# Six P.V matmuls per attention unit, and one cross product for both directions of retention

## The chip, the core and the metric

The kernel runs on one core of a Trainium2 chip. Its time is the device time of one execution, in microseconds; the number given for a kernel is the median of its runs. Five engines work side by side, each through its own instructions in order: TensorE (PE in the profile; its weight loads are shown as PEld), VectorE (DVE), ScalarE (ACT), GpSimd (POOL) and SyncE (SP). SP issues most loads. GpSimd issues nearly all stores, on its own queue, and does a little arithmetic. TensorE writes its results to PSUM, which is split into banks of 128 x 512 numbers; all other tiles lie in SBUF.

## The reference

One layer of an encoder on 1024 tokens of width 1024, in float32:

```python
x = x + 0.5 * post1(swiglu(pre1(x)))
u = pre_mix(x)
rq, rk, rv, rg, nq, nk, nv, g_ret, g_na = split(u @ w_mix_in)
y_ret = (silu(rg) * headnorm(fwd_retention + bwd_retention)) @ w_ret_out
y_na  = neighbourhood_attention(nq, nk, nv, rel_bias) @ w_na_out
x = x + post_mix((sigmoid(g_ret) * y_ret + sigmoid(g_na) * y_na) @ w_out)
x = x + 0.5 * post2(swiglu(pre2(x)))
```

Two parts matter here. **Neighbourhood attention** has 8 heads of 64 numbers on a grid of 16 rows by 64 columns of tokens; each query sees a window of 8 rows by 16 columns, with a bias, a softmax, and then P.V, the product of the probabilities with the values v. **Retention** has 4 heads (128 numbers in q and k, 256 in v). It goes through the sequence in 8 chunks of 128 tokens, forward and backward. Each direction carries a state S of 128 x 256; a chunk's output is an inner product within the chunk plus the *cross products* q.S of the two directions, each scaled by its decay.

## The kernel before

**High and low parts.** Every product is made with numbers split in two: `c.split(h, l, src)` (L62, L63) has ScalarE write the rounded high part and VectorE (or another engine given as `eng`) the rest, the low part. `c.mm3` (L92 to L96) then makes three matmuls into one bank: high.high (L94), high.low (L95), low.high (L96), so these three lines hold most of TensorE's work.

**Attention** (`na_cores`, L929) takes the heads in four pairs. A pair has 8 *units*, each a block of 8 x 16 = 128 queries with 12 x 32 = 384 keys, so there are 32 units; in the profile they run from about 973 us (the first scores) to 1145 us (the last result). A unit goes through three steps, in three consecutive turns of the loop (L1036 to L1059):

- `scores`: four matmuls (L983), the bias and the maximum (VectorE, L984, L986), the exponentials (ScalarE, L988), and the scaling by one over the sum (L990, L992).
- `flip`: `vload` brings the values of a column block when they are first needed and splits them into `vh` and `vl`, 16 times in all; six transposes (L1002) bring the keys onto the partitions, and the transposed probabilities are split into `pth` and `ptl`.
- `values`: P.V. The weights are `vh` or `vl` of one key block, 128 columns wide: 64 of the one head beside 64 of the other. The moving operand has the probabilities of both heads, 256 columns. So a matmul makes head against head, and half of its result, one head's values with the other's probabilities, isn't used. Three key blocks by three matmuls of `mm3` are nine matmuls per unit. ScalarE copies the two halves that count (64 rows each) into `ot` (L1018). After 8 units `ot` is stored to `no` in HBM.

Between these steps `fill(n)` makes the next steps of an independent generator (`products`, L1493): the projection of retention's v and the gate projections, one step being one `mm3` of 512 columns. They keep TensorE at work while a unit's softmax is made. TensorE's instructions have one order; so have the other engines'. The order on each engine is set when the program is built, by the framework's scheduler, which walks the program with a model of its times and takes the first instruction in the program's order that it thinks ready; so an instruction can stand earlier on its engine than in the text.

**Retention** (`ret_cores`, L1120) follows. Per head it walks the chunks backwards and keeps the backward states `sb` (`update`, L1167), and splits q and k (`split_qk`). Then it walks forwards: for each chunk the scores of the next (`scores`), the forward state (`update`), the split of the state (`state`), and then three groups of `mm3`: `cross[:, 256:]` with the backward state, `inner`, and `cross[:, :256]` with the forward state, each 256 columns wide. `norm` puts them together. The last chunk has no backward part and the first no forward part.

**Places.** A pool's tiles lie one behind the other in SBUF, in the order of their first mention, and pools that are opened one after another share the place. `reuse_waits="tile"` makes the first write to a new tile wait only for the old tiles that lay under it. So retention's tiles, at the place of attention's, wait for the last use of those; the lines of `pool.tile(...)` ahead of the loop (L1024 to L1032) and the `pad` tiles set which lies under which. `mix` is the pool below attention's. It holds the fill's output tiles (`ev`), the decay table `dec` and retention's gate tiles `rg`.

**The rotary part** (`rotate`, L1107), earlier in the kernel, is the one place that accumulates in HBM: it stores a tile, and then `swap` (L1115, L1116) adds other halves to it by `dma_start(..., accum_op=add)` on GpSimd's queue, which has to wait until the store has landed.

Of the kernel before, what the change touches and what calls it, by code (L numbers as in the profile page):

```python
# [19 lines left out]
P = 128  # L20
# [908 lines left out]
def na_cores(c, pool, d, bias, fill, n0, n1, n2, first, early):  # L929
# [32 lines left out]
    def vload(hp, cb):  # L962
        vr = pool.tile([P, 4, P], F32, tag="vraw", name="vraw", bufs=1)
        vh = pool.tile([P, 4, P], F32R, tag="vh", name="vh", bufs=2)
        vl = pool.tile([P, 4, P], F32R, tag="vl", name="vl", bufs=2)
        nc.sync.dma_start(vr, d["nvg"][cb][:, :, hp * P:(hp + 1) * P].rearrange("t p d -> p t d"))
        c.split(vh, vl, vr)
        vop[hp, cb] = vh, vl
# [26 lines left out]
    def flip(s):  # L995
        pth = pool.tile([P, 6, P], F32R, tag="pth", name="pth", bufs=2)
        ptl = pool.tile([P, 6, P], F32R, tag="ptl", name="ptl", bufs=2)
        for g in range(2):
            pt = c.bank("pt", 2)
            for j in range(3):  # L1000
                i = 3 * g + j
                nc.tensor.transpose(pt[:, j * P:(j + 1) * P], s[:, i % 2, (i // 2) * P:(i // 2 + 1) * P], c.ident)  # L1002
            c.split(pth[:, 3 * g:3 * g + 3], ptl[:, 3 * g:3 * g + 3],
                    pt[:, :384].rearrange("p (k t) -> p k t", k=3))
        return pth, ptl

    def values(hp, rg, cb, pt):
        if hp not in ots:
            ots[hp] = pool.tile([P, 16, 64], F32, tag="ot", name="ot", bufs=2)
        ot = ots[hp]  # L1010
        po = c.bank()
        vh, vl = vop[hp, cb]
        for k in range(3):
            c.mm3(po[:, :256].rearrange("p (e t) -> p e t", e=2), (vh[:, rg + k], vl[:, rg + k]),
                  (pt[0][:, 2 * k:2 * k + 2], pt[1][:, 2 * k:2 * k + 2]), k == 0, k == 2)
        for e in range(2):
            es = slice(64 * e, 64 * e + 64)
            nc.scalar.copy(ot[es, 8 * rg:8 * rg + 8, 16 * cb:16 * cb + 16],  # L1018
                           po[es, e * P:(e + 1) * P].rearrange("p (r c) -> p r c", c=16))
# [4 lines left out]
    for q in ("pth", "ptl"):  # L1024
        pool.tile([P, 6, P], F32R, tag=q, name=q, bufs=2)
    pool.tile([P, 4, P], F32R, tag="vl", name="vl", bufs=2)
    pool.tile([P, 128], F32, name="pad")
    qload(0)
    load(0)
    pool.tile([P, 4, P], F32R, tag="vh", name="vh", bufs=2)  # L1030
    ots[0] = pool.tile([P, 16, 64], F32, tag="ot", name="ot", bufs=2)
    pool.tile([P, 1024], F32, name="pad2")  # L1032
# [3 lines left out]
    for i in range(n + 2):  # L1036
# [17 lines left out]
        if i >= 2:  # L1054
            hp, _, rg, cb = units[i - 2]
            values(hp, rg, cb, pt.pop(i - 2))
            if (i - 2) % 8 == 7:
                c.store(d["no"][hp], ots[hp].rearrange("p r c -> p (r c)"))
# [61 lines left out]
def ret_cores(c, pool, spool, d, dec, fill, n, early):  # L1120
# [55 lines left out]
    def state(st, b):  # L1176
        s = [pool.tile([P, 256], F32R, tag=f"s{b}{q}", name=f"s{b}{q}", bufs=2) for q in "hl"]
        c.split(*s, st)
        return s
# [531 lines left out]
```

## Time and profile before

| | |
|---|---|
| median of 3 runs | 2205.85 us (2205.7 to 2206.21) |
| span of the profiled execution | 2203.7 us |
| mean granted TensorE clock | 0.999 |
| P.V matmuls (L94, L95, L96), 256 columns | 3 x 96 |
| cross product matmuls, 256 columns | 6 x 28 |
| stores of `ot` | 4, landing after 3.2 / 3.3 / 8.5 us (least, median, most) |
| loads of v (`vraw`) | 16, landing after 2.7 / 3.4 / 10.5 us |

The profiled execution's span is the time from its first to its last instruction; the median holds 2.15 us more. A line of the profile that groups instructions reads: line, engine, operation, what it writes `<-` what it reads, partitions x elements, how many | busy us, mean ns of one | idle time before them, and what ended it. A line with three numbers parted by strokes has the least, the median and the longest duration in ns and the time of the first and the last. A line of the timeline reads: start in us, duration, engine, line, operation, and in square brackets the engine's idle time before it and what ended that. A line of the waits reads: who waited, for what, us in total, times. In the busy times by stretches each engine has its busy us and, in brackets, its instructions.

### The profile page before, as it was taken

What the parts mean: (1) busy time and instruction counts of PE and PEld (TensorE: products, weight loads), DVE (VectorE), ACT (ScalarE), POOL (GpSimd) and SP (SyncE); (2) the same over time, 40 slices, a digit from 0 to 9 for tenths busy, and PEclk for the clock granted to TensorE, in tenths of its full rate; (3) what the DMA queues carried; (4) which work ended last, traced back from release to release, by engine and by line L of the source; (5) the groups of instructions that cost most, each with busy time, mean ns of one, the idle gap of its engine ahead of it and who ended that gap; (6) DMA issues with size and microseconds to landing.
All of it is one profiled execution on the core that took longest, in us unless ns stands there. A gap on an engine that the chain in (4) does not pass through costs nothing.

```text
span 2203.7 us, 29707 instructions
## 1 busy us (share of the span) xinstructions
PE 2185.3 (99%) x10232; PEld 1824.9 (83%) x10232; DVE 1573.0 (71%) x2767; ACT 959.9 (44%) x1970; POOL 585.7 (27%) x766
## 2 busy tenths in 40 slices
PE   8999999999999999999999999999999999999998
PEld 7878888888888888888888888888888888888887
DVE  7898887655568767777766677644999787866444
ACT  7444444322344332367775564322644433433232
POOL 2121222169421113311001222101112121216942
PEclk9999999999999999999999999999999999999999
DMA  7354544597745556676553466785446343549865
GB/s 264 130 200 171 203 167 169 219 375 284 247 171 188 196 172 152 155 235 180 182 171 122 154 201 220 286 305 178 148 153 229 134 167 130 181 173 374 275 225 184
DMA packets 151206, 444.63 MB, mean 202 GB/s; under 512 B 19472, under 2 KB 46224, under 8 KB 148944
## 3 DMA queue, kind: packets, MB, share of 16 engines
q1 hardware_dynamic: 107456, 298.78, 39.9%
q0 software_dynamic: 43472, 139.77, 17.8%
q10 hardware_dynamic: 128, 4.19, 0.6%
q8 instruction: 81, 1.33, 0.2%
q14 instruction: 69, 0.57, 0.1%
HBM read 294.54 MB, written 152.32 MB: 203 GB/s over the span
## 4 chain that ended last, share of the span: by engine, by line
PE 91%; issue 3%; DVE 3%; DMA 1%; ACT 1%; POOL 1%; POOLq 0%; SPq 0%; DVEq 0%; ACTq 0%
PE ps L94 28%; PE ps L95 28%; PE ps L96 28%; PE pt L96 1%; PE pt L94 1%; PE pt L95 1%; PE ps L983 1%; PE pt L1002 1%; PE pt L133 0%; POOL rstd L104 0%; DMA no<-ot 0%; PE pt L1216 0%; DMA vl<-rv 0%; DMA gt<-in_dram 0%; DMA vraw<-nvg 0%
## 5 line engine op out<-in xcount | busy, mean ns | idle before, releaser
L63 DVE TENSOR_TENSOR wl<-wraw,wh 128x512 fp32r<-128x512 f32 x440 | 294.1, 691 | 50.6 <-ACT wh L62 49.9
L62 ACT CAST wh<-wraw 128x512 fp32r<-128x512 f32 x444 | 255.2, 618 | 130.7 <-PE ps L95 58.7
L94 PE MATMUL ps<-wh,g 128*128 128x512 f32 x548 | 214.1, 391 | 0.4 <-DVE tmp L231 0.4
L95 PE MATMUL ps<-wl,g 128*128 128x512 f32 x548 | 213.6, 390 | 0.0
L96 PE MATMUL ps<-wh,g 128*128 128x512 f32 x548 | 213.3, 389 | 0.0
L63 DVE TENSOR_TENSOR wl<-w,wh 128x512 fp32r<-128x512 f32 x77 | 78.4, 1040 | 85.9 <-ACT wh L62 85.7
L63 DVE TENSOR_TENSOR wl<-x,wh 128x512 fp32r<-128x512 f32 x77 | 79.5, 1049 | 77.8 <-ACT wh L62 76.4
L62 ACT CAST wh<-t 128x512 fp32r<-128x512 f32 x58 | 36.1, 622 | 217.8 <-DVE t L575 130.6
L94 PEld LDWEIGHTS ps<-wh,g 128*128 128x128 f32 x548 | 102.9, 188 | 21.8 <-DVE tmp L231 0.7
L95 PEld LDWEIGHTS ps<-wl,g 128*128 128x128 f32 x548 | 102.9, 188 | 21.4 <-DVE wl L63 0.5
L96 PEld LDWEIGHTS ps<-wh,g 128*128 128x128 f32 x548 | 102.9, 188 | 21.3
L94 PE MATMUL ps<-a11h,wh 128*128 128x512 f32 x276 | 108.7, 395 | 1.5 <-ACT a11h L62 1.5
L94 PE MATMUL ps<-a22h,wh 128*128 128x512 f32 x280 | 109.7, 392 | 0.0
L95 PE MATMUL ps<-a11l,wh 128*128 128x512 f32 x276 | 107.9, 391 | 1.3 <-DVE a11l L63 1.3
L95 PE MATMUL ps<-a22l,wh 128*128 128x512 f32 x280 | 109.1, 390 | 0.0
L96 PE MATMUL ps<-a22h,wl 128*128 128x512 f32 x280 | 109.0, 389 | 0.0
L94 PE MATMUL ps<-a12h,wh 128*128 128x512 f32 x276 | 108.2, 393 | 0.0
L96 PE MATMUL ps<-a11h,wl 128*128 128x512 f32 x276 | 107.6, 390 | 0.0
L96 PE MATMUL ps<-a12h,wl 128*128 128x512 f32 x276 | 107.5, 390 | 0.0
L95 PE MATMUL ps<-a12l,wh 128*128 128x512 f32 x276 | 107.5, 390 | 0.0
L62 ACT CAST wh<-w 128x512 fp32r<-128x512 f32 x77 | 46.6, 620 | 112.6 <-PE pt L96 54.5
L69 POOL DMA_DIRECT2D g1a<-gth x33 | 17.8, 542 | 286.3 <-ACT gth L672 285.4
(444 smaller groups left out, 6300.6 us busy)
## 6 DMA issues: line engine op xcount, KB each, us to landing
wraw<-in_dram SPq DMA_DIRECT2D x190, 512.0 KB, 4.5
g<-g0s SPq DMA_DIRECT2D x44, 512.0 KB, 4.6
g<-g1s SPq DMA_DIRECT2D x44, 512.0 KB, 4.9
g<-g0a SPq DMA_DIRECT2D x33, 512.0 KB, 4.4
g<-g1a SPq DMA_DIRECT2D x33, 512.0 KB, 4.5
g0s<-gth POOLq DMA_DIRECT2D x44, 256.0 KB, 4.0
g0s<-cmb POOLq DMA_DIRECT2D x44, 256.0 KB, 3.9
g1s<-gth POOLq DMA_DIRECT2D x44, 256.0 KB, 3.9
```

The costliest lines, as they stand in the source:

```text
L62: self.done = [nc.scalar.copy(h, src).ins, (eng or nc.vector).tensor_tensor(l, src, hf, ALU.subtract).ins]
L63: (eng or nc.vector).tensor_tensor(l, src, hf, ALU.subtract).ins]
L69: self.nc.gpsimd.dma_start(dst, src)
L94: mm(ps, a[0], b[0], start=start, stop=False, skip_group_check=again)
L95: mm(ps, a[0], b[1], start=False, stop=False, skip_group_check=again)
L96: self.tail = mm(ps, a[1], b[0], start=False, stop=stop, skip_group_check=again).ins.name
L983: nc.tensor.matmul(bv, q[:, rg * P:(rg + 1) * P], k, start=n == 0, stop=n == 1)
L1002: nc.tensor.transpose(pt[:, j * P:(j + 1) * P], s[:, i % 2, (i // 2) * P:(i // 2 + 1) * P], c.ident)
```

## The change

Of P.V: v is split into one tile `v` of `[128, 8, 2, 64]`, in which high and low part of one head's 64 columns lie side by side, so that the weights of one matmul are [high | low] of one head; the probabilities lie the same way in `pts`, high beside low, so that the moving operand is [high | low] of that head's 128 queries. One matmul of 256 columns makes all four products of high and low; three key blocks by two heads are six matmuls. The result has v's high part on rows 0 to 63 and v's low part on rows 64 to 127, and the probabilities' low part in its own columns. The columns are added by ScalarE's copy and an addition on VectorE. The rows are added in HBM: each head's 64 upper rows are stored, and the 64 lower rows are then accumulated onto them. The low part of v is now made by GpSimd.

Of retention: the high parts of the two states lie side by side in one tile, the low parts in another, and one `mm3` of 512 columns makes both cross products, behind the inner product.

Of the places: the tiles ahead of attention's loop are listed anew, `ot` is twice as large, and `dec` and `rg` move from `mix` to a pool `late` that is opened when attention is done, at the place where attention's first tiles lay.

```diff
     def vload(hp, cb):
         vr = pool.tile([P, 4, P], F32, tag="vraw", name="vraw", bufs=1)
-        vh = pool.tile([P, 4, P], F32R, tag="vh", name="vh", bufs=2)
-        vl = pool.tile([P, 4, P], F32R, tag="vl", name="vl", bufs=2)
+        v = pool.tile([P, 8, 2, 64], F32R, tag="v", name="v", bufs=2)
         nc.sync.dma_start(vr, d["nvg"][cb][:, :, hp * P:(hp + 1) * P].rearrange("t p d -> p t d"))
-        c.split(vh, vl, vr)
-        vop[hp, cb] = vh, vl
+        c.split(v[:, :, 0], v[:, :, 1], vr.rearrange("p t (e d) -> p (t e) d", e=2), eng=nc.gpsimd)
+        vop[hp, cb] = v
...
     def flip(s):
-        pth = pool.tile([P, 6, P], F32R, tag="pth", name="pth", bufs=2)
-        ptl = pool.tile([P, 6, P], F32R, tag="ptl", name="ptl", bufs=2)
+        pts = pool.tile([P, 6, 2, P], F32R, tag="pts", name="pts", bufs=2)
...
-            c.split(pth[:, 3 * g:3 * g + 3], ptl[:, 3 * g:3 * g + 3],
-                    pt[:, :384].rearrange("p (k t) -> p k t", k=3))
-        return pth, ptl
+            c.split(*[pts[:, 3 * g:3 * g + 3, q] for q in range(2)], pt[:, :384].rearrange("p (k t) -> p k t", k=3))
+        return pts
...
     def values(hp, rg, cb, pt):
         if hp not in ots:
-            ots[hp] = pool.tile([P, 16, 64], F32, tag="ot", name="ot", bufs=2)
-        ot = ots[hp]
+            ots[hp] = pool.tile([P, 2, 16, 64], F32, tag="ot", name="ot", bufs=2)
         po = c.bank()
-        vh, vl = vop[hp, cb]
-        for k in range(3):
-            c.mm3(po[:, :256].rearrange("p (e t) -> p e t", e=2), (vh[:, rg + k], vl[:, rg + k]),
-                  (pt[0][:, 2 * k:2 * k + 2], pt[1][:, 2 * k:2 * k + 2]), k == 0, k == 2)
+        v = vop[hp, cb]
         for e in range(2):
-            es = slice(64 * e, 64 * e + 64)
-            nc.scalar.copy(ot[es, 8 * rg:8 * rg + 8, 16 * cb:16 * cb + 16],
-                           po[es, e * P:(e + 1) * P].rearrange("p (r c) -> p r c", c=16))
+            for k in range(3):
+                nc.tensor.matmul(po[:, 256 * e:256 * e + 256], v[:, 2 * (rg + k) + e].rearrange("p q d -> p (q d)"),
+                                 pt[:, 2 * k + e].rearrange("p q t -> p (q t)"), start=k == 0, stop=k == 2)
+        po = po.rearrange("p (e q r c) -> p e q r c", e=2, q=2, r=8)
+        ot = ots[hp][:, :, 8 * rg:8 * rg + 8, 16 * cb:16 * cb + 16]
+        for e in range(2):
+            nc.scalar.copy(ot[:, e], po[:, e, 1])
+        for e in range(2):
+            nc.vector.tensor_tensor(ot[:, e], po[:, e, 0], ot[:, e], ALU.add)
...
-    for q in ("pth", "ptl"):
-        pool.tile([P, 6, P], F32R, tag=q, name=q, bufs=2)
-    pool.tile([P, 4, P], F32R, tag="vl", name="vl", bufs=2)
-    pool.tile([P, 128], F32, name="pad")
+    pool.tile([P, 6, 2, P], F32R, tag="pts", name="pts", bufs=2)
+    pool.tile([P, 8, 2, 64], F32R, tag="v", name="v", bufs=2)
+    pool.tile([P, 4, P], F32, tag="vraw", name="vraw", bufs=1)
+    pool.tile([P, 512], F32, name="pad")
     qload(0)
     load(0)
-    pool.tile([P, 4, P], F32R, tag="vh", name="vh", bufs=2)
-    ots[0] = pool.tile([P, 16, 64], F32, tag="ot", name="ot", bufs=2)
-    pool.tile([P, 1024], F32, name="pad2")
+    ots[0] = pool.tile([P, 2, 16, 64], F32, tag="ot", name="ot", bufs=2)
...
             if (i - 2) % 8 == 7:
-                c.store(d["no"][hp], ots[hp].rearrange("p r c -> p (r c)"))
+                for e in range(2):
+                    o = ots[hp][:, e].rearrange("p r c -> p (r c)")
+                    c.store(d["no"][hp][64 * e:64 * e + 64], o[:64])
+                    nc.gpsimd.dma_start(d["no"][hp][64 * e:64 * e + 64], o[64:], accum_op=ALU.add)
...
-    def state(st, b):
-        s = [pool.tile([P, 256], F32R, tag=f"s{b}{q}", name=f"s{b}{q}", bufs=2) for q in "hl"]
-        c.split(*s, st)
-        return s
+    def states():
+        return [pool.tile([P, 2, 256], F32R, tag=f"s{q}", name=f"s{q}", bufs=2) for q in "hl"]
...
-            if cc < NC - 1:
-                c.mm3(cross[:, 256:], q, sbs, True, True)
             c.mm3(inner, a, v, True, True)
-            if cc > 0:
-                c.mm3(cross[:, :256], q, sf, True, True)
+            bs = slice(0 if cc > 0 else 1, 2 if cc < NC - 1 else 1)
+            c.mm3(cross.rearrange("p (b d) -> p b d", b=2)[:, bs], q, [p[:, bs] for p in now], True, True)
...
-    mix.tile([P, 104], F32, name="pad")
     evpool[:] = [mix]
...
-    tabs = mix.tile([P, 536], F32, name="dec")
+    late = pool(m_stack, "late")
+    late.tile([P, 104], F32, name="pad")
+    tabs = late.tile([P, 536], F32, name="dec")
...
-        ret_cores(c, ret, mix, d, dec, fill, RET_FILL, early)
+        ret_cores(c, ret, late, d, dec, fill, RET_FILL, early)
```

More of the change, by code (lines that the diff above doesn't have):

```diff
@@ L1241, in ret_cores @@
         a = scores(h, ops, 0)
-        v, sbs, st, sf = vget(0), state(sb[:, 0], "b"), None, None
+        v, st, now = vget(0), None, states()
+        c.split(*[q[:, 1] for q in now], sb[:, 0])
         fill(n[4])
@@ L1250, in ret_cores @@
             q = [o[:, cc * P:(cc + 1) * P] for o in ops["q"]]
-            nsf = None
+            nxt = states() if cc < NC - 1 else None
             if cc < NC - 1:
@@ L1254, in ret_cores @@
                 update(h, 0, kf, cc, v, old, st)
-                nsf = state(st, "f")
+                c.split(*[p[:, 0] for p in nxt], st)
             cross, inner = c.bank(), c.bank()[:, :256]
-            if cc < NC - 1:
-                c.mm3(cross[:, 256:], q, sbs, True, True)
             c.mm3(inner, a, v, True, True)
-            if cc > 0:
-                c.mm3(cross[:, :256], q, sf, True, True)
+            bs = slice(0 if cc > 0 else 1, 2 if cc < NC - 1 else 1)
+            c.mm3(cross.rearrange("p (b d) -> p b d", b=2)[:, bs], q, [p[:, bs] for p in now], True, True)
             left.append((h, cc, norm(h, cc, cross, inner)))
@@ L1265, in ret_cores @@
             if cc < NC - 2:
-                sbs = state(sb[:, cc + 1], "b")
+                c.split(*[p[:, 1] for p in nxt], sb[:, cc + 1])
             fill(n[6])
@@ L1270, in ret_cores @@
             fill(n[7])
-            a, sf = b, nsf
+            a, now = b, nxt
     for e in left:
```

## The prediction

> **What bounds the kernel now.** I read the page first, for the engine that is full, then the busy time by stretches of the stage that changes (neighbourhood attention, about 973 to 1145 us), then single instructions there.
>
> ```profile
> span 2203.7 us, 29707 instructions
> PE 2185.3 (99%) x10232; PEld 1824.9 (83%) x10232; DVE 1573.0 (71%) x2767; ACT 959.9 (44%) x1970; POOL 585.7 (27%) x766
> PE 91%; issue 3%; DVE 3%; DMA 1%; ACT 1%; POOL 1%; POOLq 0%; SPq 0%; DVEq 0%; ACTq 0%
> ```
>
> TensorE is busy for 99% of the span and makes 91% of the chain that ended last. The other engines matter only where TensorE would come to wait for them, so the stage has to be looked at by itself. The columns are PE, PEld, DVE, ACT and POOL busy time, granted clock, DMA share, GB/s.
>
> ```profile
> 980.00:1020.00 40.00, 39.79 (x231) 34.42 (x230) 32.18 (x91) 30.59 (x83) 7.67 (x8) 1.00 0.62 185
> 1020.00:1060.00 40.00, 40.00 (x242) 35.70 (x241) 35.01 (x101) 33.42 (x90) 5.38 (x7) 1.00 0.73 241
> 1060.00:1100.00 40.00, 40.00 (x242) 35.74 (x241) 28.78 (x92) 26.85 (x79) 2.19 (x4) 1.00 0.48 143
> 1100.00:1140.00 40.00, 40.00 (x237) 35.47 (x236) 30.83 (x90) 32.39 (x84) 3.22 (x6) 1.00 0.45 151
> ```
>
> TensorE is full in all of them, at the full clock (1.00). VectorE is second: 126.8 us of 160 in the first four, 35.0 of 40 in the second. So removed matmuls are worth their whole time, as long as VectorE keeps up.
>
> **What a matmul costs.** The durations of matmuls overlap, so I take the distance from start to start.
>
> ```profile
> 983.71 0.28 PE L94 MATMUL ps<-pth,vh 128*128 128x256 f32 x1
> ...
> 984.42 0.40 PE L94 MATMUL ps<-wh,a12h 128*128 128x512 f32 x1
> ```
>
> ```profile
> 1146.24 0.39 PE L94 MATMUL ps<-a12h,wh 128*128 128x512 f32 x1
> ...
> 1151.68 0.39 PE L94 MATMUL ps<-a22h,wh 128*128 128x512 f32 x1
> ```
>
> Six P.V matmuls of 256 columns lie between the first two rows: 0.71 / 6 = 0.118 us each. Twenty-four matmuls of 512 columns lie between the last two: 5.44 / 24 = 0.227 us. Two narrow ones thus cost 0.009 us more than one wide one.
>
> ```profile
> L94 PE MATMUL ps<-pth,vh 128*128 128x256 f32 x96 | 29.5, 307 | 0.0
> L94 PE MATMUL ps<-sbh,qh 128*128 128x256 f32 x28 | 8.1, 289 | 0.8 <-DVE y L1199 0.8
> ```
>
> **The change, part by part.** *P.V.* 96 calls on L94, as many on L95 and L96, are 288 matmuls, nine for each of 32 units. Six remain of the same width (128 weight columns, 256 moving columns). 32 x 3 x 0.118 = 11.4 us of TensorE go, all on the path.
>
> *Retention's cross product.* The backward part is computed for 28 chunks (seven of each head's eight: the last has none), the forward part for as many (the first has none), so 24 chunks have both. There six matmuls of 256 become three of 512: 24 x 3 x 0.009 = 0.7 us. Its operands are made in the same steps as before; the inner product only moves in front of it. No new wait.
>
> Together 12.1 us of TensorE. What follows is what may be given back.
>
> *More for VectorE, less for it, and a new tenant on GpSimd.*
>
> ```profile
> L63 DVE TENSOR_TENSOR vl<-vraw,vh 128x512 fp32r<-128x512 f32 x16 | 11.0, 687 | 0.3 <-ACT vh L62 0.2
> L1018 ACT COPY ot<-ps 64x128 f32<-64x128 f32 x64 | 16.7, 261 | 0.7 <-PE ps L96 0.3
> ```
>
> ```profile
> L1187 DVE TENSOR_TENSOR a<-ps,dec x32: 280/282/292, 1173.5 to 1371.6; 128x128 f32<-128x128 f32 x32
> L63 POOL TENSOR_TENSOR k<-kraw,k x6: 1279/1338/1622, 982.2 to 1055.8; 64x512 fp32r<-64x512 f32 x6
> L986 DVE TENSOR_SCALAR nast<-nast x32: 158/166/1286, 975.1 to 1133.7; 128x2 f32<-128x2 f32 x32
> ```
>
> ScalarE's two copies per unit stay: 128 rows in place of 64 at the same length, so 0.261 us each, nothing added. VectorE gets two additions of 128x128 per unit, PSUM plus SBUF; L1187 has just that shape: 64 x 0.282 = 18.0 us. It loses the sixteen low-part splits of v, 11.0 us. These go to GpSimd, whose nearest row is the split of k: 16 x 1.338 = 21.4 us. GpSimd has room, but it holds VectorE up: the third row, a step of 0.166 us, once took 1.286, and of the next three rows the first and last show the same on splits from SBUF, while the middle one, of splits that read PSUM, never left 536 to 558 ns.
>
> ```profile
> 1051.66 2.38 DVE L63 TENSOR_TENSOR wl<-wraw,wh 128x512 fp32r<-128x512 f32 x2
> ```
>
> ```profile
> L63 DVE TENSOR_TENSOR ptl<-pt,pth x64: 536/550/558, 981.3 to 1141.2; 128x384 fp32r<-128x384 f32 x64
> ```
>
> ```profile
> 1052.18 1.32 POOL L63 TENSOR_TENSOR k<-kraw,k 64x512 fp32r<-64x512 f32 x1 [11.65 <-ACT k L62]
> ```
>
> Two splits of 0.69 us took 2.38 us while GpSimd split k, about 1.0 us more than 2 x 0.69. So the 21.4 us of new GpSimd work cost VectorE between 0 (when it does work that reads PSUM, or nothing) and 21.4 us. I take the middle, 10.7 us: VectorE's work there alternates between the two kinds. VectorE then needs 126.8 + 18.0 - 11.0 + 10.7 = 144.5 us, in a stage that TensorE would now do in 160 - 11.4 = 148.6 us: 97%. By stretch: with some 7.7 units in each (32 units from 973 to 1145 us, 5.3 us each, rounded up), each gets 7.7 x (17.7 / 32) = 4.3 us more, and TensorE 2.7 us less: 36.5, 39.3, 33.1 and 35.1 us against 37.3. The second is over by 2.0. In front of it there is a cushion or there is none:
>
> ```profile
> 987.07 0.75 DVE L992 TENSOR_SCALAR s<-s,narc 128x384 f32<-128x384 f32 x2
> ```
>
> ```profile
> 1073.63 0.75 DVE L992 TENSOR_SCALAR s<-s,narc 128x384 f32<-128x384 f32 x2
> ```
>
> ```profile
> 987.92 0.82 PE L1002 MATMUL pt<-ident,s 128*128 128x128 f32 x6
> ```
>
> ```profile
> 1077.48 0.82 PE L1002 MATMUL pt<-ident,s 128*128 128x128 f32 x6
> ```
>
> The probabilities are ready 0.1 us ahead of their transposes at 987.8 and 3.1 us ahead at 1074.4. So the first stretch, short of slack already, keeps perhaps 1 us less of its gain, and the second loses its 2.0. With no hold-up by GpSimd the loss is 0; with all of it each stretch gets 2.6 us more, and the excess is 1.8 + 4.6 + 0 + 0.4 = 6.8 us. I take 3.0 us, near the middle.
>
> By the Trainium skill (SBUF — State Buffer, section "SBUF: two separate sides") VectorE and GpSimd share a port pair under an exclusive lock, and whichever comes second blocks fully; only VectorE work in a two-port mode or with two SBUF inputs is concerned. The rows above agree in kind, and by that rule alone the additions from PSUM are safe; at its fullest it makes the loss 6.8 instead of 3.0 us, which is a rival below.
>
> *The last head's result.* Each head pair's store of 512 KB becomes two stores and two accumulating DMAs on GpSimd's queue. The nearest rows are those of the rotary part, which stores and then accumulates in the same way.
>
> ```profile
> L1115 POOL DMA_DIRECT2D rk<-evt x8: 842/860/892, 816.0 to 931.9; - x8
> L1116 POOL DMA_DIRECT2D rk<-evt x8: 996/1137/1163, 816.6 to 932.4; - x8
> ...
>   DMA rk<-ev: 38.3, 8
> ```
>
> ```profile
> DMA to landing us min/median/max: 3.0/3.2/6.3
> ```
>
> There GpSimd waited 38.3 us in 8 times, 4.8 us each, for the store, issuing two took 0.86 + 1.14 us, and the accumulating ones of L1115 (the second fence is theirs) landed after 3.2 us, at most 6.3. Behind that wait stand GpSimd's other work: the splits of v and k and the stores of the fill products. For three of the four head pairs, 2 x 4.8 + 2.0 + 1.1 = 12.7 us of queue at most come where the next split of v is two units (10 us) and its reader three units off: hidden, and if the cover is gone, P.V waits the 1 to 3 us by which it is late. The fourth is different, since the next stage's tiles lie where it was.
>
> ```profile
> 1146.03 8.52 DMA no<-ot
> ```
>
> ```profile
> 1154.77 1.29 DVE L63 TENSOR_TENSOR kl<-kraw,kh 128x512 fp32r<-128x512 f32 x2 [1.77 <-DMA no<-ot]
> ...
> 1157.85 0.68 DVE L63 TENSOR_TENSOR vl<-vl,vh 128x512 fp32r<-128x512 f32 x1
> ```
>
> ```profile
> 1173.49 0.29 DVE L1187 TENSOR_TENSOR a<-ps,dec 128x128 f32<-128x128 f32 x1 [1.72 <-PE ps L96]
> ```
>
> ```profile
> 1158.58 0.39 PE L95 MATMUL ps<-vl,kdh 128*128 128x256 f32 x1 [0.48 <-DVE vl L63]
> ```
>
> Retention's split of k (kl) waits for that landing, and behind it on VectorE stands vl, for which TensorE waits already. The change's tiles cover the same places for kl and both halves of q. If all transfers land in 3.2 us, kl is free no later than now (0.5 + 0.5 + 3.2 + 2.0 + 3.2 = 9.4 against 0.5 + 8.5): 0. If the stores land in 8.5 as here and the additions in 6.3, it is 0.5 + 0.5 + 8.5 + 2.0 + 6.3 = 17.8, 8.8 us later. Each of these microseconds is TensorE's if kl keeps its place ahead of vl; but kl itself is needed only for the scores at 1173.5, so a planner that knows of the later landing can set it behind. I take 1.0 us: about 4 us late, one time in four on the path.
>
> *The decay table and the gate tiles* go to a pool whose place the probability tiles held.
>
> ```profile
> L1530 SPq DMA_DIRECT2D dec<-dec x1: 383/383/383, 978.8 to 978.8; - x1
> L65 ACT ACTIVATE kdh<-ps,dec x16: 667/686/694, 1155.9 to 1329.8; 128x512 fp32r<-128x512 f32 x16
> ```
>
> The table's load went out at 978.8; now it must wait for the last units' P.V, and so until about 1145 on the old clock, the end of attention. Landing in some 4 us like its neighbours, it is there 7 us ahead of its first reader at 1155.9. On SP's queue it stands ahead of retention's own loads, which wait for the last P.V in any case. 0; if the cover went, its lateness would stop ScalarE and then TensorE.
>
> **The sum.** 11.4 + 0.7 - 3.0 - 1.0 = 8.1 us off the profiled execution's 2203.7: 2195.6. The median of the runs is 2205.85, 2.15 us longer than the profiled span, so 2197.7 us.
>
> **The rivals.** *Clean:* VectorE's work fits and nothing is late. For it: the third stretch, with 3 us in hand. Against: 35.0 of 40 in the second. 2205.85 - 12.1 = 2193.7. Chance 0.22.
>
> *VectorE blocked for the whole of GpSimd's new work:* the loss is 6.8 instead of 3.0, 2201.5. For it: the 1.286 us row, nearly a whole GpSimd instruction. Against: much of VectorE's work in the stage reads PSUM. Chance 0.08. The lock that the Trainium skill describes (SBUF — State Buffer, "SBUF: two separate sides"), at its fullest, is this case.
>
> *The stage change on the path:* kl stays ahead of vl and is 8.8 us late. 12.1 - 3.0 - 8.8 leaves 0.3 us: 2205.5, no change. For it: kl stands ahead of vl now, with 0.48 us of TensorE waiting. Chance 0.12.
>
> *Slower:* at the same place the four transfers go strictly one after another, each with 8.52 us to land, the issues 0.5 + 0.86 + 0.5 + 1.14. That is 37.1 us against 9.0, kl is 28 us late, and TensorE stands for it: 2205.85 - 12.1 + 28 = 2221.8. It decides from the point where kl is over 12.1 us later than now. For it: the store then runs beside the new stage's loads, the reason of the 8.52. Against: by the second pair those loads are over. Chance 0.08.
>
> *The matmuls removed were hidden:* six would have to take as long as nine. Nothing speaks for it but that weights are 83% busy; their loads fall from nine to six as well. 2205.9, chance 0.02.
>
> **How the numbers follow.** My forecast, 2195.5 to 2200, has 0.48. A measurement of this kernel can tell 0.2%, 4.4 us, from no change: under 2201.4 is faster, over 2210.3 slower. Faster: 0.48 + 0.22 + half of the blocked case 0.04 = 0.74. Slower: 0.08. The rest, 0.18, is the same. The range goes from the clean case with 0.7 us of margin (TensorE's present wait of 0.48 us could go too), 2193.0, to the stage change on the path, 2205.5.
>
> **What the next profile would show.** Right: 192 P.V matmuls 0.118 us apart, 10,064 matmuls in all; VectorE over 90% in its second stretch; waits of TensorE for VectorE of 2 to 4 us between 980 and 1140; the accumulating DMA of `no` landing some 4 us later, relative to the last P.V, than the store did, with kl behind vl. Wrong: transposes or P.V waiting for v from GpSimd, or a TensorE gap of over 3 us at the stage change ended by the landing of `no`; or P.V matmuls further apart than 0.118 us.

## The result, and the profile after

The changed kernel is slower, by a little but clear of the scatter: 2213.74 us, median of 5 runs (2211.97 to 2215.38), against 2205.85 us (2205.7 to 2206.8, 5 runs). The ratio is 1.0036, 95% interval 1.0025 to 1.0048. The forecast was 2197.7 us, in a range from 2193.0 to 2205.5.

The page of the changed kernel first: the same lines as were shown of the kernel before.

```profile
span 2210.2 us, 29546 instructions
PE 2179.2 (99%) x10064; PEld 1812.8 (82%) x10064; DVE 1581.6 (72%) x2815; ACT 952.4 (43%) x1970; POOL 619.1 (28%) x794
PE 90%; DVE 4%; issue 3%; DMA 1%; POOL 1%; ACT 1%; SPq 0%; POOLq 0%; DVEq 0%; ACTq 0%
```

The 168 matmuls are gone (10232 to 10064), and yet TensorE's share of the chain fell and VectorE's rose from 3% to 4%. TensorE waits more. The groups show that the work itself is as it was meant to be: 192 P.V matmuls, and 24 joined cross products of 512 columns for each of the three lines of `mm3`.

```profile
L1011 PE MATMUL ps<-pts,v 128*128 128x256 f32 x192 | 31.8, 300 | 0.0
L94 PE MATMUL ps<-sh,qh 128*128 128x512 f32 x24 | 10.0, 415 | 1.0 <-DVE y L1197 0.9
```

Six of the first kind take 0.71 us from start to start in the chain of waits, 0.118 each, so TensorE's work did become 12.1 us shorter. Where did more than that go? The stretches of attention, as before (PE, PEld, DVE, ACT and POOL busy, granted clock, DMA share, GB/s):

```profile
980.00:1020.00 40.00, 36.47 (x202) 31.69 (x202) 33.79 (x96) 29.17 (x83) 14.31 (x13) 0.96 0.56 166
1020.00:1060.00 40.00, 40.00 (x230) 35.34 (x229) 34.58 (x112) 31.38 (x92) 11.86 (x12) 1.00 0.75 241
1060.00:1100.00 40.00, 38.22 (x216) 32.73 (x215) 33.28 (x106) 25.77 (x78) 13.01 (x14) 1.00 0.59 163
1100.00:1140.00 40.00, 40.00 (x232) 35.30 (x231) 33.25 (x107) 32.94 (x92) 9.43 (x12) 1.00 0.56 171
```

TensorE has holes in the first and the third stretch, and VectorE isn't full in either. To have one measure for all kernels I take, for every matmul, the distance to the start of the next one, less what its width takes in an undisturbed row (0.109, 0.119, 0.178 and 0.227 us for 128, 256, 384 and 512 columns), and add up what is left. This is TensorE's lost time, whether it stood or ran slowly:

| lost, us | attention, 960 to 1140 | stage change, 1140 to 1180 | retention, 1180 to 1340 | elsewhere |
|---|---|---|---|---|
| before | 2.7 | 1.1 | 3.7 | 10.5 |
| after | 10.1 | 7.3 | 7.6 | 11.6 |
| forecast of the increase | 3.0 | 1.0 | 0 | 0 |
| increase | 7.3 | 6.2 | 3.9 | 1.1 |

The increases make 18.6 us, against 12.1 us saved (7.3 + 6.2 + 3.9 + 1.1 is 18.5 by the rounded figures): 6.5 us longer, as the spans say (2210.2 - 2203.7). In the first stretch the loss is 5.8 us (1.4 before), in the third 3.3 (0.4); in the second and the fourth it is 0.4, as before.

Lost time is read from one profiled execution of a kernel, whose time lies up to 2.4 us from the kernel's median. A difference of a microsecond or two between two kernels says little by itself; it counts where several kernels repeat it.

**Attention.** TensorE's waits between 960 and 1400 us, longest first (who, for what: us, times, longest), then VectorE's instructions, GpSimd's and TensorE's around one of them:

```profile
PE ps L94 <- ACT vh L62: 4.5, 1, 4.5
PE pt L1000 <- DVE s L991: 4.1, 4, 1.5
PE ps L94 <- DVE y L1197: 1.8, 3, 0.9
```

```profile
1010.40 1.26 DVE L985 TENSOR_SCALAR nast<-nast 128x2 f32<-128x2 f32 x1
...
1014.53 2.64 DVE L991 TENSOR_SCALAR s<-s,narc 128x384 f32<-128x384 f32 x2
```

```profile
1014.35 1.26 POOL L63 TENSOR_TENSOR v<-vraw,v 128x512 fp32r<-128x512 f32 x1 [2.71 <-ACT v L62]
1015.69 1.26 POOL L63 TENSOR_TENSOR k<-kraw,k 64x512 fp32r<-64x512 f32 x1
```

```profile
1015.97 0.30 PE L1000 MATMUL pt<-ident,s 128*128 128x128 f32 x1 [1.49 <-DVE s L991]
1017.22 1.33 PE L1000 MATMUL pt<-ident,s 128*128 128x128 f32 x5 [0.95 <-DVE s L991]
```

The two scalings of the probabilities, 0.75 us in the kernel before, take 2.64 us here, just as long as GpSimd takes for its splits of v and then of k. The transposes wait for them. By the groups, it is single instructions that are held up, the median isn't (ns: least, median, longest):

```profile
L991 DVE TENSOR_SCALAR s<-s,narc x64: 407/418/1526, 979.4 to 1136.0; 128x384 f32<-128x384 f32 x64
```

```profile
L985 DVE TENSOR_SCALAR nast<-nast x32: 155/164/1265, 976.2 to 1132.5; 128x2 f32<-128x2 f32 x32
```

**Stage change.** The chain of waits there:

```profile
1143.28 1.11 POOL no L69 x2
1144.38 7.40 issue
1151.80 1.34 POOL no L1058 x2
1153.20 5.49 DMA sn<-ev
...
1159.70 0.68 DVE kl L63
1160.38 1.32 DVE kdl L66 x2
```

Two stores, 7.4 us until they have landed, two accumulating transfers, 5.5 us more, and then `kl`, which was not set behind anything: `kdl` and `vl` stand behind it. (The 5.49 us are put down to `sn<-ev`, a store that GpSimd issued right behind the accumulating ones; `kl` itself has to wait for `ot`, on which it lies, as e4 below bears out.) TensorE's rows:

```profile
1157.45 0.47 PE L96 MATMUL ps<-a12h,wl 128*128 128x512 f32 x1
1162.38 0.79 PE L94 MATMUL ps<-vh,kdh 128*128 128x256 f32 x2 [4.45 <-ACT vh L62]
...
1165.27 0.63 PE L95 MATMUL ps<-a21l,wh 128*128 128x512 f32 x1
1165.70 0.63 PE L96 MATMUL ps<-a21h,wl 128*128 128x512 f32 x1
```

It stands for 4.45 us until `vh` is there. On ScalarE `vh` stands behind a `kdh` that waited 1.94 us for VectorE's `kdl`, and that stood behind `kl`. Then TensorE runs at half speed: the last two rows start 0.43 us apart, where 512 columns take 0.227.

### The profile page after: what moved, and what is told of

Read it like the earlier page. It is cut to its first block, busy times and chain, and to the rows that moved or that the text cites. A ratio compares the mean times of both kernels' runs of the same rounds, so it can differ in the third digit from the quotient of the medians.

```text
span 2210.2 us, 29546 instructions
## 1 busy us (share of the span) xinstructions
PE 2179.2 (99%) x10064; PEld 1812.8 (82%) x10064; DVE 1581.6 (72%) x2815; ACT 952.4 (43%) x1970; POOL 619.1 (28%) x794
## 4 chain that ended last, share of the span: by engine, by line
PE 90%; DVE 4%; issue 3%; DMA 1%; POOL 1%; ACT 1%; SPq 0%; POOLq 0%; DVEq 0%; ACTq 0%
PE ps L94 27%; PE ps L95 27%; PE ps L96 27%; PE pt L96 1%; PE pt L95 1%; PE pt L94 1%; PE ps L1011 1%; PE pt L1000 1%; PE ps L982 1%; PE pt L133 0%; POOL rstd L104 0%; DVE s L991 0%; DVE wl L63 0%; DMA vl<-rv 0%; DMA gt<-in_dram 0%
```

## The experiments

The lost time of each kernel, as above, and its time. Ratios are to the kernel before on the same chip; the kernels were not all measured on one chip. Each excerpt of code shows only the lines that matter (`...` stands for others).

| kernel | attention | stage change | retention | time, us | ratio (95%) |
|---|---|---|---|---|---|
| e1: joined cross product alone | 2.5 | 1.2 | 11.9 | 2215.36 | 1.0038 (1.0023 to 1.0053) |
| e5: cross products apart, behind inner | 2.3 | 1.3 | 5.3 | 2208.65 | 1.0009 (1.0 to 1.0019) |
| e6: joined, ahead of inner | 2.5 | 1.4 | 5.7 | 2206.61 | 1.0001 (0.9992 to 1.0011) |
| e2: the change without the joined product | 13.4 | 7.7 | 4.9 | 2212.66 | 1.0024 (1.0014 to 1.0034) |
| e3: the change, v split on VectorE | 7.3 | 8.5 | 6.7 | 2208.54 | 1.0009 (0.9999 to 1.0018) |
| e10: before, v split on GpSimd | 9.1 | 1.3 | 4.0 | 2212.68 | 1.0028 (1.0019 to 1.0038) |
| e4: the change, `ot` last | 12.5 | 5.1 | 10.0 | 2213.54 | 1.0025 (1.0015 to 1.0035) |
| e7: P.V mended | 7.0 | 2.8 | 3.7 | 2204.82 | 0.9992 (0.9982 to 1.0001) |
| e8: the same without the additions | 8.5 | 2.8 | 5.5 | 2204.66 | 0.999 (0.998 to 0.9999) |
| e11: e7 with the table late | 11.8 | 5.2 | 4.5 | 2210.76 | 1.0021 (1.0011 to 1.003) |
| e9: e7, k split on VectorE as well | 3.0 | 2.8 | 4.7 | 2199.37 | 0.9972 (0.9959 to 0.9984) |
| e12: all mended, joined ahead of inner | 2.9 | 4.4 | 4.3 | 2196.08 | 0.9953 (0.994 to 0.9967) |

**e1, the joined cross product alone**, put into the kernel before with the change's own lines for it:

```diff
...
-            if cc < NC - 1:
-                c.mm3(cross[:, 256:], q, sbs, True, True)
             c.mm3(inner, a, v, True, True)
-            if cc > 0:
-                c.mm3(cross[:, :256], q, sf, True, True)
+            bs = slice(0 if cc > 0 else 1, 2 if cc < NC - 1 else 1)
+            c.mm3(cross.rearrange("p (b d) -> p b d", b=2)[:, bs], q, [p[:, bs] for p in now], True, True)
...
```

> Only retention's cross product is joined; attention, its places and its stores are as before. In the changed kernel retention (1180 to 1380 us) has 8.1 us of TensorE idle or slow time against 4.2 before. If the joined product itself makes TensorE wait (it stands behind the inner product and needs both states at once), this kernel is about 2.5 to 3.5 us slower than before: some 2209 us. If retention's loss in the changed kernel comes from what attention leaves behind (a different phase of loads and fill steps), this kernel gains its 0.7 us: some 2205 us.

It costs 8.7 us by itself, over twice what was expected. Rows of the kernel before and of e1, from the end of one chunk's cross product to the start of the next:

```profile
1252.04 0.28 PE L96 MATMUL ps<-sfh,ql 128*128 128x256 f32 x1
...
1253.76 0.48 DVE L1199 SCALAR_TENSOR_TENSOR y<-ps,dec,y 128x256 f32<-128x256 f32 x1
...
1255.82 0.28 PE L94 MATMUL ps<-sbh,qh 128*128 128x256 f32 x1
```

```profile
1253.29 0.39 PE L96 MATMUL ps<-sh,ql 128*128 128x512 f32 x1
...
1256.53 0.39 ACT L62 CAST sh<-st 128x256 fp32r<-128x256 f32 x1
1256.82 0.47 ACT L1195 ACTIVATE y<-ps,dec 128x256 f32<-128x256 f32 x1
...
1257.63 0.48 DVE L1197 SCALAR_TENSOR_TENSOR y<-ps,dec,y 128x256 f32<-128x256 f32 x1
...
1258.16 0.50 PE L94 MATMUL ps<-sh,qh 128*128 128x512 f32 x1 [0.43 <-DVE y L1197]
```

Before, `y` has read its bank 1.6 us ahead of the next cross product (1254.24 against 1255.82). In e1 ScalarE comes to `y` only behind the split of the next state, 3.5 us after the cross product, and TensorE waits until VectorE's half of `y` is done. Over the 24 chunks that have both directions, VectorE's read begins 3.2 us (median) after the start of the last cross matmul, against 2.0 before, and the next cross product starts within 0.2 us of its end, or is waiting for it, 8 times against 3. Not all of e1's loss is this, though. TensorE's two largest waits between 1160 and 1390 us:

```profile
PE ps L94 <- DVE y L1197: 2.7, 4, 1.0
PE ps L94 <- ACT ev L1486: 2.3, 1, 2.3
```

The kernel before waits 0.8 us for `y` there, once. The 2.3 us are a wait of the inner product for the bank of a fill result (`ev`): on ScalarE its copy stood behind the split of a v that had not landed.

Is it the joining, or the place behind the inner product? **e5** moves only the order, **e6** joins in front (shown against e1):

```diff
+            c.mm3(inner, a, v, True, True)
             if cc < NC - 1:
                 c.mm3(cross[:, 256:], q, sbs, True, True)
-            c.mm3(inner, a, v, True, True)
             if cc > 0:
                 c.mm3(cross[:, :256], q, sf, True, True)
```

> The kernel before, with its two cross products still apart (three matmuls of 256 columns each), but both behind the inner product. Theory (joining): the joined product waits because it needs the whole bank and both directions' states at once; the order alone moves the first cross product 0.36 us later, which gives its bank's last reader (y) more room. Then no difference: 2204 to 2208 us, and the loss of TensorE in 1240 to 1340 us stays at about 3 us. Rival (order): the cross product that comes later makes y later, and y later holds the bank of the next chunk. Then most of the 8.6 us that the joined product alone cost: 2211 to 2215 us.

```diff
-            c.mm3(inner, a, v, True, True)
             bs = slice(0 if cc > 0 else 1, 2 if cc < NC - 1 else 1)
             c.mm3(cross.rearrange("p (b d) -> p b d", b=2)[:, bs], q, [p[:, bs] for p in now], True, True)
+            c.mm3(inner, a, v, True, True)
```

> The kernel before with the joined cross product ahead of the inner product. Theory (joining): it still needs the bank and both states at once, and needs them 0.36 us earlier: slower than before by 6 to 10 us, 2212 to 2216 us. Rival (order): with the cross product in front, y can be read early and the loss goes: 2204 to 2207 us.

I expected e6 to be slow, and it isn't: the loss needs both, joined and behind. Apart and behind costs 1.9 us (interval 0 to 4.2), joined in front nothing that can be told. The retention column repeats it: the four kernels with the joined product behind (e1, e3, e4 and the change) lose 6.7 to 11.9 us there, all others 3.7 to 5.7.

How the loss comes about is seen only in part. Banks are given out by the order in which they are first written and come free. In the programs as built, with the cross product in front, its tile takes over the bank of a state update in 18 of 32 chunks (before and e6); behind the inner product it takes over the bank of the previous chunk's cross product in 19 of 32 (e1 and e5), so it has to wait for that chunk's `y`. That alone doesn't tell the kernels apart: with the cross product in front it is the inner product that takes over the previous cross product's bank, in 18 chunks (before) and 19 (e6). Counting both products, 25 take over such a bank in each of the four kernels. What differs is how early `y` is done. In e1 ten of the 25 start within 0.2 us of the end of `y` or wait for it, in the kernel before 3, in e6 one, in e5 4; TensorE's idle time in front of them is 2.7 us in e1, 0.8 before, 0 in e6 and 0.9 in e5. So late `y` explains some 2 us of the 8.2 that e1 loses more, and the wait for `ev` another 2.3; the rest is shorter waits, among them 0.6 us for the split state (`sh`, `sl`), and slow stretches, whose cause was not tested. e5 has the same banks as e1, and there `y` reads under 2 us (median) after the last cross matmul, in e1 3.2. That `y` is set later when the joined product stands behind is observed; why was not tested.

**e2, the change without the joined product** (its lines in `ret_cores` taken back, the rest kept):

```diff
...
+            if cc < NC - 1:
+                c.mm3(cross[:, 256:], q, sbs, True, True)
             c.mm3(inner, a, v, True, True)
-            bs = slice(0 if cc > 0 else 1, 2 if cc < NC - 1 else 1)
-            c.mm3(cross.rearrange("p (b d) -> p b d", b=2)[:, bs], q, [p[:, bs] for p in now], True, True)
+            if cc > 0:
+                c.mm3(cross[:, :256], q, sf, True, True)
...
```

> The whole change except the joined cross product: retention is as before. If the joined product costs what the changed kernel loses in retention, this is about 3 us faster than the changed kernel, some 2210 to 2211 us. If it costs nothing, it is 0.7 us slower than the changed kernel, some 2214 us. In both cases the 7 us lost in attention and the 6 us at the change of stage stay.

Retention's loss goes back by 2.7 us, the other two losses stay. So P.V's part loses more than its 11.4 us by itself. The order on the engines is planned anew for each program, and attention's loss scatters by some 3 us with it (10.1 and 13.4 for the same code there).

**e3, the low part of v on VectorE again:**

```diff
-        c.split(v[:, :, 0], v[:, :, 1], vr.rearrange("p t (e d) -> p (t e) d", e=2), eng=nc.gpsimd)
+        c.split(v[:, :, 0], v[:, :, 1], vr.rearrange("p t (e d) -> p (t e) d", e=2))
```

> The changed kernel with the low part of v made by VectorE again, sixteen operations of 0.69 us. If GpSimd's sixteen operations hold VectorE up (scalings of 0.75 us for two that took 2.64 and 2.14 us), attention's idle TensorE time between 980 and 1080 us falls from about 9.3 us to 3 or less, and the kernel to some 2207 us. If it is VectorE's total work that is too much (the additions), 11 us more of it makes it worse: 2215 us or more.

VectorE gets 11 us more to do, and the kernel becomes 5 us faster than the change. But attention's loss falls only from 10.1 to 7.3 us, not to 3 or less; the rest is found in e9. The converse, **e10, the kernel before with v's low part on GpSimd and nothing else**:

```diff
-        c.split(vh, vl, vr)
+        c.split(vh, vl, vr, eng=nc.gpsimd)
```

> The kernel before with one edit: the low part of v is made by GpSimd. VectorE has 11 us less to do, GpSimd some 21 us more. Theory (GpSimd's splits hold VectorE up): VectorE's small steps and scalings from SBUF stretch where they meet a split, and TensorE's loss in 960 to 1140 us grows from 2.7 to 5 or 7 us: 2208 to 2211 us. Rival (only VectorE's own work counts): no loss, 2205 to 2207 us.

This one edit costs 6.5 us, though it takes work from VectorE. TensorE's waits from 960 to 1140 us, and the step of 0.166 us that was already seen at 1.286 in the kernel before:

```profile
PE pt L1002 <- DVE ptl L63: 2.8, 4, 1.6
PE ps L94 <- ACT ev L1397: 1.3, 1, 1.3
```

```profile
L986 DVE TENSOR_SCALAR nast<-nast x32: 153/166/1269, 975.2 to 1140.2; 128x2 f32<-128x2 f32 x32
```

`ptl` itself, which reads PSUM, is never long here (541 to 558 ns). It stands on VectorE behind steps that are, among them four of this `nast` step, five splits of q and three of k; the way from each of them to a wait was not followed.

**e4, `ot` last in attention's pool,** so that retention's kl, qh and ql don't lie on it (it is the change with the tiles of q, the bias and the scores claimed ahead of `ot`):

```diff
     load(0)
+    for e in range(2):
+        for q in "hl":
+            pool.tile([P, 16, 16], F32R, tag=f"q{e}{q}", name=f"q{q}", bufs=2)
+    for q in ("bt", "s"):
+        pool.tile([P, 2, 384], F32, tag=q, name=q, bufs=2)
     ots[0] = pool.tile([P, 2, 16, 64], F32, tag="ot", name="ot", bufs=2)
```

> The changed kernel with the result tiles of attention as the last in its pool, so that retention's high and low parts of k and q lie under tiles that are free early, and the results' place is used only by tiles that are written some 10 us later. If the gap of 4.7 us at 1157 us is the wait of k's split for the accumulating DMAs, it goes, with the slow clock behind it: 6 us, some 2207.5 us. If something else of the change of stage is late too (the decay table, the loads), a gap of 2 us or more stays: 2210 us or more.

```profile
1154.69 1.29 DVE L63 TENSOR_TENSOR kl<-kraw,kh 128x512 fp32r<-128x512 f32 x2 [0.30 <-ACT kh L62]
```

```profile
1158.29 1.04 PE L1166 MATMUL ps<-ident,kraw 128*128 128x128 f32 x8
1159.08 0.47 PE L96 MATMUL ps<-a12h,wl 128*128 128x512 f32 x1
1162.01 0.50 PE L94 MATMUL ps<-vh,kdh 128*128 128x256 f32 x2 [2.46 <-ACT vh L62]
```

`kl` no longer waits, but a gap of 2.46 us stays, and the kernel is no faster than the change: what the stage change gains (7.3 to 5.1), attention and retention lose (2.4 us each), though none of their code differs. I put it down to the first two of TensorE's rows: the eight transposes of k stand behind all but one of the fill matmuls, so hardly anything is left to cover the splits that follow them. Hence **e7**: P.V's part with v's split on VectorE, `ot` last, no joined product, and the decay table back in `mix`, loaded early (the gate tiles stay in `late`, since there isn't room for both):

```diff
...
+    mix.tile([P, 104], F32, name="pad")
     evpool[:] = [mix]
...
-    late = pool(m_stack, "late")
-    late.tile([P, 104], F32, name="pad")
-    tabs = late.tile([P, 536], F32, name="dec")
+    tabs = mix.tile([P, 536], F32, name="dec")
     c.after(nc.sync.dma_start(tabs, d["dec"]).ins, early)
     dec = Decays(tabs)
     fill.until("rv")
+    late = pool(m_stack, "late")
```

> P.V in six matmuls, with the low part of v on VectorE, the result tiles of attention last in their pool (so that the split of retention's k and q doesn't lie on them), the decay table back in its old pool and loaded early, and the cross products as in the kernel before. TensorE has 11.4 us less to do. If each of the three losses has the cause that I gave it, the stage change goes back from 7.3 to about 1 us of loss, retention to 3, and attention keeps the 4.5 us over the kernel before that were left with v on VectorE: 2205.9 - 11.4 + 4.5 = 2199 us. If the decay table's load has no part in the transposes' late place, the stage change keeps the 4 us that were left with the result tiles moved alone: 2203 us. If the loss is due to something else altogether (for instance the accumulating transfers as such): 2207 us or more.

```profile
1152.35 1.03 PE L1165 MATMUL ps<-ident,kraw 128*128 128x128 f32 x8
1153.14 0.47 PE L95 MATMUL ps<-a12l,wh 128*128 128x512 f32 x1
...
1154.15 0.39 PE L96 MATMUL ps<-a12h,wl 128*128 128x512 f32 x1
1155.96 0.50 PE L94 MATMUL ps<-vh,kdh 128*128 128x256 f32 x2 [1.43 <-ACT vh L62]
```

Five fill matmuls now stand behind the transposes instead of one, and the loss falls from 5.1 to 2.8. **e11** is e7 with the table and the gate tiles in `late` again, as in the change:

```diff
...
-    tabs = mix.tile([P, 536], F32, name="dec")
+    late = pool(m_stack, "late")
+    late.tile([P, 104], F32, name="pad")
+    tabs = late.tile([P, 536], F32, name="dec")
...
```

> The mended P.V kernel, with the decay table and the gate tiles again in the late pool, as in the change, so that the table is loaded only when attention's last probability tile has been used, ahead of retention's own loads. Theory (the table's load moves the transposes): the eight transposes of k come some 4 us later after the last P.V than in the mended kernel (there 1152.35, about 14 us behind it), with no fill steps left behind them, and the loss in 1140 to 1180 us goes from 2.9 to 5 to 7 us: 2207 to 2209 us. Rival (the place of the result tiles was all): it stays at about 3 us, 2204 to 2206 us.

The loss at the stage change is 5.2 again, so the late table costs some 2.4 us there. The levels repeat: 7.3, 7.7 and 8.5 with `ot` in front and the table late (the change, e2, e3), 5.1 and 5.2 with `ot` last (e4, e11), 2.8 three times with both mended (e7, e8, e9; e12 has 4.4). The expected 4 us of delay were wrong: from the start of the last unit's P.V to the transposes it is 16.2 us here and 15.3 in e7. Of the 5.9 us between the two kernels the rest is not explained by the stage change: attention's start (960 to 1000 us) loses 5.8 us here and 1.6 in e7, 2.3 of it in one wait of the scores for VectorE's split of k. Whether the table has a part in that is open.

e7 was 2204.8 where 2199 was hoped for: attention kept its loss. Is VectorE too full? **e8** is e7 without the additions (and so without the product of the probabilities' low part):

```diff
         for e in range(2):
-            nc.scalar.copy(ot[:, e], po[:, e, 1])
-        for e in range(2):
-            nc.vector.tensor_tensor(ot[:, e], po[:, e, 0], ot[:, e], ALU.add)
+            nc.scalar.copy(ot[:, e], po[:, e, 0])
```

> The kernel above, without the 64 additions on VectorE: ScalarE copies the columns of the probabilities' high part, and those of the low part are left out of the result. If VectorE's fuller stage is what makes TensorE wait in attention with v's split on VectorE, that loss falls by 4 to 5 us against the kernel above, to about 2 us: 2194 to 2195 us. If the waits come from GpSimd's remaining splits of k, or from the new order, it stays: within 1.5 us of the kernel above.

No gain: 18 us less for VectorE, and attention loses 8.5 instead of 7.0 us; the times agree (2204.66 and 2204.82). So it isn't the amount of VectorE's work. **e9** is e7 with GpSimd's last splits (of k) given to VectorE:

```diff
-                c.split(kop[hp][e][es, bs], kop[hp][e][es_, bs], kr[es, bs], eng=nc.gpsimd if hp and b else None)
+                c.split(kop[hp][e][es, bs], kop[hp][e][es_, bs], kr[es, bs])
```

> The mended P.V kernel (low part of v on VectorE, result tiles last, decay table early, cross products as before) with the low part of k on VectorE as well, so that GpSimd does no arithmetic in attention. Theory (GpSimd's splits hold VectorE up): TensorE's loss in 960 to 1140 us, 7.0 us in the mended kernel, goes back to about the 2.7 us of the kernel before, and no scaling of the probabilities takes over 0.8 us for two: 2200 to 2202 us. Rival (VectorE is simply too full): it gets 6 x 0.68 = 4.1 us more work, so the loss stays or grows: 2205 to 2208 us.

```profile
980.00:1020.00 40.00, 40.00 (x232) 34.83 (x231) 36.99 (x117) 32.85 (x93) 3.42 (x6) 1.00 0.64 187
1020.00:1060.00 40.00, 40.00 (x231) 35.33 (x230) 37.04 (x121) 31.86 (x95) 3.95 (x6) 1.00 0.84 244
1060.00:1100.00 40.00, 39.39 (x228) 34.49 (x227) 35.46 (x117) 27.75 (x85) 6.21 (x10) 1.00 0.67 185
```

```profile
L991 DVE TENSOR_SCALAR s<-s,narc x64: 401/415/536, 979.3 to 1128.5; 128x384 f32<-128x384 f32 x64
```

Here VectorE is fuller in each of these stretches than in the kernels before and after, 93% in the second, and TensorE is nearly whole again. The longest scaling takes 0.536 us. The loss of attention is about that of the kernel before (3.0 and 2.7), and the kernel beats it by 0.28%. Since e9 keeps the additions and the accumulating transfers, neither of them is what made TensorE wait in attention.

A count over all these kernels says which instructions matter: VectorE's, started between 960 and 1140 us, that took over 0.1 us longer than the median of their group, and by how much together. Each of them ran beside a split on GpSimd, but for the one in e9.

| kernel | splits on GpSimd | held up | above the median, us | lost in attention, us |
|---|---|---|---|---|
| before | k | 3 | 3.2 | 2.7 |
| after | k and v | 9 | 8.1 | 10.1 |
| e10 | k and v | 14 | 10.6 | 9.1 |
| e3 | k | 5 | 4.6 | 7.3 |
| e7 | k | 5 | 4.6 | 7.0 |
| e8 | k | 5 | 4.5 | 8.5 |
| e9 | none | 1 | 0.1 | 3.0 |
| e12 | none | 0 | 0 | 2.9 |

**e12** puts the joined product of e6 into e9:

```diff
...
-            if cc < NC - 1:
-                c.mm3(cross[:, 256:], q, sbs, True, True)
+            bs = slice(0 if cc > 0 else 1, 2 if cc < NC - 1 else 1)
+            c.mm3(cross.rearrange("p (b d) -> p b d", b=2)[:, bs], q, [p[:, bs] for p in now], True, True)
             c.mm3(inner, a, v, True, True)
-            if cc > 0:
-                c.mm3(cross[:, :256], q, sf, True, True)
```

> The whole change with its losses mended: six P.V matmuls, no split by GpSimd in attention, result tiles last, decay table early, and the joined cross product, but ahead of the inner product. TensorE has 12.1 us less to do than in the kernel before; the same kernel with the cross products apart took 2199.4. If joining in front costs what it saves, as it did alone: 2199 to 2201 us. If joining in front gains its 0.7 us here: 2197.5 to 2199 us. If the joined product waits as it did behind the inner product: 2203 us or more.

2196.08 us, the fastest of all, and by 0.47% faster than the kernel before. Against e9, measured on another chip, that is 3.3 us less by the medians, but the intervals overlap, so what the joined product is worth here isn't settled. The stage change still loses 4.4 us.

## Why the prediction was wrong

**TensorE's saving** was right: 192 P.V matmuls at 0.118 us, 24 x 3 of 512 columns, 12.1 us of work gone. e12, which keeps all of it and loses little, is 10.3 us faster than the kernel before.

**"No new wait" for the cross product** failed. The working looked at the operands of the product, not at its place in TensorE's order nor at the bank that it writes. Joined and behind costs 8.7 us by itself (e1), in the change 3.9 of lost time (2.7 of it go when the product is taken apart again, e2); the place ahead of the inner product takes it away (e6). That the pair of joining and place costs this is shown. How is shown in part: waits for the late `y`, the reader of a bank's old contents, are some 2 us of e1's 8.2, and the rest stays open.

**VectorE and GpSimd.** The mechanism was named, the size was wrong, and its form too. I priced GpSimd's hold-up as more VectorE work, so that only the excess of the fullest stretch would be lost: 3.0 us, at most 6.8. It was 7.3. The fullest stretch (1020 to 1060 us), where 2.0 of the 3.0 were put, lost no more than before, with VectorE at 86% and not over 90%; the first and the third lost the 7.3. And the hold-up was less than the 10.7 us assumed, 8.1 against 3.2 before. The two experiments with opposite signs decide: less work for VectorE and more for GpSimd loses (e10, 6.4 us of lost time more), more for VectorE and none for GpSimd doesn't (e9). What counts is not whether VectorE's work fits into the stretch but which instruction is held up: the scalings stand between the softmax and the transposes, and the delay of 1.9 us at 1014 is TensorE's at once. The even spreading over each stretch hid that. The additions from PSUM were safe, as assumed (in the change 0.269 to 0.292 us each).

A part of this loss was in no term at all. With six P.V matmuls and the splits of k and v on GpSimd, attention loses 10.1 to 13.4 us (the change, e2, e4); with k's alone 7.0 to 8.5 (e3, e7, e8; 11.8 in e11 with its loss at the start); with neither 2.9 and 3.0 (e9, e12). So some 3 us of the change's loss belong to v's splits and some 4 to k's, which GpSimd made in the kernel before too, without a loss to be seen. They may hurt now because TensorE has 11.4 us less work to cover them with; that was not tested.

By the Trainium skill (SBUF — State Buffer, section "SBUF: two separate sides") VectorE and GpSimd hold their shared ports exclusively, for a whole instruction, when VectorE's instruction is in a two-port mode or has two SBUF inputs. The trace agrees: a step of 0.164 us took 1.265 and a scaling of 0.418 us 1.526, each 1.1 us more, within the 1.26 us of one GpSimd split; the additions with a PSUM operand never did. Whether these steps were in such a mode the trace doesn't tell.

**The stage change** was put at 1.0 us, on the ground that a planner that knows of the later landing can set `kl` behind `vl`. It didn't: `kl` kept its place, and the loss is 6.2 us. That is the rival "the stage change on the path", chance 0.12, with 8.8 us. Three parts were found: the landing (7.3 to 5.1 with `ot` elsewhere, e4), the table's late load, which I had put at 0 because its reader was 7 us away (about 2.4, e7 and e11), and a rest of some 1.7 us over the kernel before that remains in e7 and was not explained. The row for the accumulating transfers, 3.2 us to landing, was that of L1115 alone; L1116's, of the same kind, had a median of 4.1 and a longest of 12.8, and the change's took 4.1 to 6.3. The table's price isn't that its reader waits. With the table late, the transposes come later and the fill work is used up ahead of them; I take this for the planner's doing, but how it weighs that load was not tested.

**A term that was not in the sum** is what a gap costs after its end: the slow clock, below. It is part of the lost times above.

The likeliest case, 2195.5 to 2200 us, would have needed all three estimates to hold; each was low, and they added up to 17.4 us instead of 4.0. The one rival that was called slower had another mechanism, four transfers one after the other and `kl` 28 us late; here the two stores overlapped, and so did the two additions.

## What to carry to other kernels

When work moves off a busy engine, ask which instructions of that engine run beside the new place and who waits for them; a stage where the engine's total fits can still lose, and one where it is 93% full can be whole. When a matmul is moved or made wider, look at the bank that it writes as at an operand: who reads the old contents, and how late. And try the new shape in the old place before it is given up: joined in front cost nothing. Memory that a long chain of transfers frees last should lie under the tiles that the next stage needs last, and a load moved from early to late costs through the order of the fill work even when its reader never waits.

## What the runs showed of the hardware

After a gap TensorE doesn't come back at full speed. The stretches behind the stage change of the changed kernel (columns as above):

```profile
1157.00:1162.00 5.00, 0.93 (x8) 0.62 (x6) 2.91 (x5) 2.75 (x5) 0.00 (x0) 0.79 0.41 105
1162.00:1167.00 5.00, 4.18 (x13) 3.47 (x14) 4.50 (x8) 3.85 (x8) 0.00 (x0) 0.52 0.77 238
1167.00:1172.00 5.00, 5.00 (x28) 4.30 (x27) 2.95 (x6) 0.62 (x1) 0.00 (x0) 1.00 0.51 192
```

The granted clock (the third number from the end) is 0.52 for the 5 us behind the gap of 4.45 us, and full again after that. So the 4.45 us cost another 2 us or so. The Trainium skill (TensorE: Matmul & The Clock Gate, "Part 1: The HAM clock gate") has the clock fall to one half after an idle window of about 3.4 us, and gives 426.7 ns between matmuls of 512 columns then; the 0.43 us here agree. But shorter gaps do it as well: behind the waits of 1.49 and 0.95 us at 1016, six P.V matmuls took 1.43 us from start to start, 0.24 each instead of 0.118, with a granted clock of 0.57 between 1016 and 1020 us:

```profile
1018.20 1.63 PE L1011 MATMUL ps<-pts,v 128*128 128x256 f32 x6
1019.63 0.56 PE L94 MATMUL ps<-wh,a22h 128*128 128x512 f32 x1
```
